# A transpose through TensorE: sixteen ranges with gathered stores in place of eight ranges with direct ones

## The chip, the cores and the metric

The kernel runs on one core of one Trainium2 chip. The metric is the time of one execution on the device, in microseconds; 1264.57 us is the median of 3 runs of the kernel before. Engines are named as in the profile: PE is TensorE (matmuls and transposes, which write PSUM), DVE is VectorE, ACT is ScalarE, POOL is GpSimd, SP is SyncE. DMA engines, 16 of them, move data between main memory (HBM) and the core's own memory (SBUF); SP and ACT issue such transfers, and an engine that issues one does not wait for it.

## The reference

```python
x = np.random.randn(8192, 8192).astype(np.float32)

def reference(x):
    return np.transpose(x)
```

Every float32 of a matrix of 268 MB is read once and written once, and nothing is computed.

## The kernel before

The input is cut into chunks of 128 rows by 4096 columns (2 MiB): `s` is the half of the columns, `c` one of `CH` = 64 groups of rows, and `chunks` lists the `T` = 128 of them, all groups of the first half and then of the second. A load (`load`, L100) brings one chunk to SBUF: 128 partitions, each a 16 KB row of `x`. There are `NIN` = 3 input buffers.

PE turns a chunk into 32 blocks of 128x128 (`transposes`, L111). One transpose takes every fourth column of a range of 512 columns (`B` = 4), so that output partition p holds the output rows 4p to 4p + 3 of that range. A chunk has `NR` = 8 ranges; their results fill PSUM, ranges 0 to 3 in half 0 and 4 to 7 in half 1. PE's program is a loop (L135 to L150) of three chunks a turn, 96 transposes in the code, with semaphores that are counted down.

ACT copies half 0 from PSUM to SBUF, DVE half 1 (L228). They copy straight into the place from which the range will be stored. An output row of 8192 floats is written in pieces, and a piece is longer the more chunks one waits for: each range is collected over `W` = 8 chunks into a region of 16 KB a partition, holding four output rows of 1024 floats, that is 4 KB. The windows of the eight ranges are staggered, so that one range closes in every chunk (`span`, L194) and one store of 2 MiB goes out. Of `NREG` = 9 regions eight are being filled, and one is free or being stored. A window that runs over the end of the first half of the columns is stored in two parts; at the start and the end windows are cut short. These partial stores are of 256 KB to 1792 KB.

`store` (L160) issues on ACT, as `load` does from chunk 3 on (L102): ACT waits until the closing copies are done, issues the store, waits until PE is through with the chunk (L242), and issues the load of three chunks ahead into the buffer that has come free. All DMAs but the first three loads thus stand in ACT's queue, in the order in which ACT reaches them. `wide_dma` (L25) writes the store as an instruction whose source is one contiguous run of 16 KB per partition, while its destination has four rows. PE waits for the load (`s_ld`) and for each PSUM half (`s_bank`); a copy waits for PE (`s_pe`) and, where it opens a window, for the store that last used its region (`s_st`).

Of the kernel before, what the change touches and what calls it, by code (L numbers as in the profile page):

```python
# [24 lines left out]
def wide_dma(nc, eng, queue, out, in_):  # L25


    return eng.add_instruction(
        mybir.InstDMACopy(
            mode="Copy",  # L30
            name=nc.get_next_instruction_name(),
            engine=eng.engine,
            ins=[physical(in_)],
            outs=[physical(out)],
            queue=queue,
        )
    )
# [3 lines left out]
def kernel(  # L41
# [10 lines left out]

    nc = tc.nc
    P = 128
    N, M = x.shape
    assert x.shape == out.shape[::-1]
    dt = x.dtype

    S = 32
    B = 4
    W = 8
    NR = S // B
    NIN = 3
    NREG = 9
    CH = N // P
    J = S * P

    with tc.tile_critical():  # L70
        nc.alloc_sbuf_tensor("pad", [P, 32], dt)
        ident = nc.alloc_sbuf_tensor("ident", [P, P], dt).ap()
        ins = [nc.alloc_sbuf_tensor(f"in{k}", [P, J], dt).ap() for k in range(NIN)]
        SIZE = B * W * P
        regs = nc.alloc_sbuf_tensor("regs", [P, NREG * SIZE], dt).ap()
        NH = NR // 2
        pss = [nc.alloc_psum_tensor(f"ps{k}", [P, NH * B * P], dt).ap() for k in range(2)]

        s_id = nc.alloc_semaphore("s_id")
        s_ld = [nc.alloc_semaphore(f"s_ld{k}") for k in range(NIN)]  # L80
        s_st = [nc.alloc_semaphore(f"s_st{k}") for k in range(NREG)]
        s_bank = [nc.alloc_semaphore("s_banka"), nc.alloc_semaphore("s_bankv")]
        s_pe = nc.alloc_semaphore("s_pe")
        s_cp = [nc.alloc_semaphore("s_cpa"), nc.alloc_semaphore("s_cpv")]

        nc.gpsimd.memset(ident, 0.0).then_inc(s_id, 1)  # L86
        nc.gpsimd.wait_ge(s_id, 1)
# [1 line left out]
            out=ident,  # L89
# [5 lines left out]
            channel_multiplier=1,  # L95
        ).then_inc(s_id, 1)

        chunks = [(s, c) for s in range(M // J) for c in range(CH)]

        def load(t):  # L100
            s, c = chunks[t]
            (nc.sync if t < NIN else nc.scalar).dma_start(  # L102
                out=ins[t % NIN], in_=x[c * P:(c + 1) * P, s * J:(s + 1) * J]
            ).then_inc(s_ld[t % NIN], 16)

        def transposes(k):  # L111
            nc.tensor.sem_inc(s_ld[k], -16).wait_op(s_ld[k], 16, "sem-ge")
            for q in range(NR):
                e, g = divmod(q, NH)
                if g == 0:
                    nc.tensor.sem_inc(s_bank[e], -1).wait_op(s_bank[e], 1, "sem-ge")  # L116
                for b in range(B):
                    tr = nc.tensor.transpose(  # L118
                        pss[e][:, (g * B + b) * P:(g * B + b + 1) * P],
                        ins[k][:, q * B * P + b:(q + 1) * B * P - B + b + 1:B],  # L120
                        ident,
                    )
                if q % 2:
                    tr.then_inc(s_pe, 1)

        T = len(chunks)
        assert T % NIN == NIN - 1
        pe = [nc.tensor.engine]  # L130
        for e in range(2):
            nc.tensor.sem_inc(s_bank[e], 1)
        nc.tensor.wait_ge(s_id, 2)

        turn = nc.alloc_registers("turn", engines=pe)  # L135
        nc.regs_mov(turn, 0)
        nc.br("turns", engines=pe)
        with nc.body("turns", valid_engines=pe):
            now = nc.snap(turn, min_val=0, max_val=T // NIN)
            with nc.tensor.If(now < 3):  # L140
                hint = nc.tensor.mark_branch_hint_location()
            with nc.tensor.If(now > 0):
                transposes(NIN - 1)
            for k in range(NIN - 1):
                transposes(k)
            nc.regs_alu(turn, turn, 1, op=mybir.AluOpType.add)
            nc.tensor.br_lt(
                turn, T // NIN + 1, on_true="turns", on_false="done"
            ).branch_hint(hint)
        nc.switch_bb("done")  # L150

        for t in range(NIN):
            load(t)

        copied = [0, 0]
        free = list(range(NREG))
        stored = [0] * NREG
        window = {}

        def store(q, e, count):  # L160
            t0, r, parts = window.pop(q)
            nc.scalar.wait_ge(s_cp[e], count)
            base = 0
            for s, a, z in parts:
                rows = (z - a) * P
                j0 = s * J + q * B * P
                dst = out[j0:j0 + B * P, a * P:a * P + rows]
                dst = dst.rearrange("(q b) i -> q b i", q=P)
                src = regs[:, r * SIZE + base:r * SIZE + base + B * rows]
                base += B * rows  # L170
                if any(stored):
                    st = wide_dma(nc, nc.scalar, "qActDynamicHW", dst, src)
                else:
                    st = nc.scalar.dma_start(
                        out=dst, in_=src.rearrange("q (b i) -> q b i", b=B)
                    )
                st.then_inc(s_st[r], 16)
                stored[r] += 1
            free.append(r)

        def closes(w, t):
            t0, r, parts = w
            return t + 1 == t0 + sum(z - a for _, a, z in parts)

        for t, (s, c) in enumerate(chunks):
            for e in range(2):
                eng = (nc.scalar, nc.vector)[e]

                place = []
                for q in range(e * NH, (e + 1) * NH):  # L190
                    if q not in window:

                        span = (q - c) % W + 1
                        r = free.pop(0)
                        parts = [(s, c, min(c + span, CH))]
                        if c + span > CH and t + span < T:
                            parts.append((s + 1, 0, c + span - CH))
                        window[q] = (t, r, parts)  # L200
                        if stored[r]:
                            eng.wait_ge(s_st[r], 16 * stored[r])
                    t0, r, parts = window[q]
                    k = [p[0] for p in parts].index(s)
                    base = r * SIZE + B * P * sum(z - a for _, a, z in parts[:k])
                    _, a, z = parts[k]
                    place.append((base + (c - a) * P, (z - a) * P))

                runs = []
                for g in range(NH):  # L210
                    if runs:
                        u = runs[-1]
                        gap = place[g][0] - place[g - 1][0]
                        if place[g][1] == place[u[0]][1] and abs(gap) < 2 ** 15 and (
                            len(u) == 1 or gap == place[u[1]][0] - place[u[0]][0]
                        ):
                            u.append(g)
                            continue
                    runs.append([g])
                for u in runs:  # L220
                    off, dist = place[u[0]]
                    gap = place[u[-1]][0] - place[u[-2]][0] if len(u) > 1 else 0
                    dims = [list(regs.ap[0]), [gap, len(u)], [dist, B], [1, P]]
                    o = bass.AP(regs.tensor, regs.offset + off, dims)
                    i = pss[e][:, u[0] * B * P:(u[-1] + 1) * B * P]
                    i = i.rearrange("p (l b i) -> p l b i", b=B, i=P)
                    eng.wait_ge(s_pe, t * NH + (e * NH + u[-1]) // 2 + 1)  # L227
                    cp = nc.scalar.copy(out=o, in_=i) if e == 0 else nc.vector.tensor_copy(out=o, in_=i)  # L228
                    ends = [e * NH + g for g in u if closes(window[e * NH + g], t)]
                    if ends:  # L230
                        cp.then_inc(s_cp[e], 1)
                        copied[e] += 1
                    if u is runs[-1]:
                        if ends:
                            eng.wait_ge(s_cp[e], copied[e])
                            eng.sem_inc(s_bank[e], 1)
                        else:
                            cp.then_inc(s_bank[e], 1)
                    for q in ends:
                        store(q, e, copied[e])  # L240
            if t + NIN < T:
                nc.scalar.wait_ge(s_pe, (t + 1) * NR // 2)  # L242
                load(t + NIN)
        for r in range(NREG):
            nc.sync.wait_ge(s_st[r], 16 * stored[r])


# [28 lines left out]
```

## Time and profile before

| what | value |
|---|---|
| runs | 1263.68 to 1264.68 us, median 1264.57 |
| the profiled execution's span | 1261.2 us |
| HBM read, written | 268.44 MB each |
| loads: 3 issued by SP, 125 by ACT | 2048 KB each |
| stores | 114 of 2048 KB, and 4 each of 1792, 1536, 1280, 1024, 768, 512 and 256 KB |
| PE transposes | 4096, mean granted clock 0.751 of full speed |
| copies PSUM to SBUF | 256 on ACT, 250 on DVE, of 512 to 2048 columns |

The span runs from the first to the last instruction of one execution that was profiled; the runs time the whole execution. In a row of a group of instructions stand the busy time, the mean duration of one in ns, the idle time of the engine before them, and what ended it. Engine rows of a timeline give the start, the length, and how many were merged.

### The profile page before, as it was taken

What the parts mean: (1) busy time and instruction counts of PE and PEld (TensorE: products, weight loads), DVE (VectorE), ACT (ScalarE), POOL (GpSimd) and SP (SyncE); (2) the same over time, 40 slices, a digit from 0 to 9 for tenths busy, and PEclk for the clock granted to TensorE, in tenths of its full rate; (3) what the DMA queues carried; (4) which work ended last, traced back from release to release, by engine and by line L of the source; (5) the groups of instructions that cost most, each with busy time, mean ns of one, the idle gap of its engine ahead of it and who ended that gap; (6) DMA issues with size and microseconds to landing.
All of it is one profiled execution on the core that took longest, in us unless ns stands there. A gap on an engine that the chain in (4) does not pass through costs nothing. (4 is left out here: it accounts for less than half of the span.)

```text
span 1261.2 us, 9840 instructions
## 1 busy us (share of the span) xinstructions
PE 740.3 (59%) x4096; PEld 719.8 (57%) x4096; DVE 302.7 (24%) x250; ACT 252.6 (20%) x257; POOL 0.7 (0%) x6
## 2 busy tenths in 40 slices
PE   6555655665556565665555655656566655656561
PEld 6555555665556555655555655656566655656561
DVE  3322222222222222222222222222222222222220
ACT  3212121121111211122211121121111211122120
POOL 0000000000000000000000000000000000000000
PEclk9987867777776868687776777676867677777866
DMA  9999999999999999999999999999999999999998
GB/s 386 429 427 426 430 427 429 431 428 430 431 428 431 429 429 430 430 429 430 425 423 419 431 430 429 430 430 429 431 430 429 431 429 430 430 430 429 429 429 351
DMA packets 39273, 536.97 MB, mean 426 GB/s; under 512 B 4320, under 2 KB 4832, under 8 KB 6240
## 3 DMA queue, kind: packets, MB, share of 16 engines
q10 hardware_dynamic: 38832, 530.60, 98.9%
q1 hardware_dynamic: 432, 6.29, 1.2%
q14 instruction: 8, 0.07, 0.0%
q8 instruction: 1, 0.02, 0.0%
HBM read 268.44 MB, written 268.44 MB: 426 GB/s over the span
## 5 line engine op out<-in xcount | busy, mean ns | idle before, releaser
L118 PE MATMUL ps<-ident,in 128*128 128x128 f32 x4096 | 740.3, 363 | 492.9 <-PEq L116 492.9
L118 PEld LDWEIGHTS ps<-ident,in 128*128 128x128 f32 x4096 | 719.8, 220 | 513.2 <-issue 513.2
L228 DVE COPY regs<-ps 128x512 f32<-128x512 f32 (+3 forms) x250 | 302.7, 1246 | 932.4 <-PE ps L118 780.2
L228 ACT COPY regs<-ps 128x512 f32<-128x512 f32 (+3 forms) x256 | 251.3, 1015 | 980.9 <-PE ps L118 495.5
L228 ACT ACT_TABLE_LOAD x1 | 1.3, 1283 | 0.9 <-SPq L70 0.9
L88 POOL TENSOR_SCALAR_AFFINE_SELECT ident<-ident 128x128 f32<-128x128 f32 x1 | 0.3, 292 | 0.2 <-POOL ident L86 0.2
L86 POOL MEMSET ident<- 128x128 f32 x1 | 0.2, 204 | 0.5 <-SPq L70 0.5
L260 POOL MEMSET const-bfloat16-1.0<- 128x1 bf16 x1 | 0.1, 101 | 0.0
L260 POOL MEMSET const-uint8-127<- 128x1 uint8 x1 | 0.1, 101 | 0.0
L260 POOL MEMSET const-float32-0.0<- 128x1 f32 x1 | 0.1, 98 | 0.2 <-issue 0.2
L260 POOL MEMSET const-float32-1.0<- 128x1 f32 x1 | 0.1, 98 | 0.0
## 6 DMA issues: line engine op xcount, KB each, us to landing
in<-in_x_dram ACTq DMA_DIRECT2D x125, 2048.0 KB, 21.7
out_dram<-regs ACTq DMA_DIRECT2D x114, 2048.0 KB, 17.5
out_dram<-regs ACTq DMA_DIRECT2D x4, 1792.0 KB, 17.1
in<-in_x_dram SPq DMA_DIRECT2D x3, 2048.0 KB, 11.6
out_dram<-regs ACTq DMA_DIRECT2D x4, 1536.0 KB, 15.2
out_dram<-regs ACTq DMA_DIRECT2D x4, 1280.0 KB, 15.5
out_dram<-regs ACTq DMA_DIRECT2D x4, 1024.0 KB, 15.6
out_dram<-regs ACTq DMA_DIRECT2D x4, 768.0 KB, 16.5
```

What stands on the lines that cost most here:

```text
L86: nc.gpsimd.memset(ident, 0.0).then_inc(s_id, 1)
L88: nc.gpsimd.affine_select(out=ident, in_=ident, compare_op=mybir.AluOpType.not_equal, fill=1.0, base=0, pattern=[[-1, P]], channel_multipl ...
L118: tr = nc.tensor.transpose(pss[e][:, (g * B + b) * P:(g * B + b + 1) * P], ins[k][:, q * B * P + b:(q + 1) * B * P - B + b + 1:B], ident,)
L228: cp = nc.scalar.copy(out=o, in_=i) if e == 0 else nc.vector.tensor_copy(out=o, in_=i)
L260: nc = _bacc.Bacc("TRN2", target_bir_lowering=False, num_devices=1)
```

## The change

There are now 16 ranges of 256 columns (`B` = 2, `W` = 16): output partition p holds output rows 2p and 2p + 1 of a range, and a store's rows are of 8 KB. Each range is collected over 16 chunks.

- SBUF holds five units of 16 KB a partition (`units`): two input buffers (`NIN` = 2) and three from which ranges are stored (`NF` = 3). The third of these takes the load of chunk 2 and joins the others for window 4.
- Pieces that wait for their range are kept in 120 `slots` of 1 KB a partition. The slots form a triangle: where piece (chunk t, range q) lay, the piece (q, t) is put once the first has been gathered.
- PE takes the ranges of chunk t in the order t, t + 1, ... modulo 16. So the first piece belongs to the range that closes now, the second to the one that closes with the next chunk.
- ACT copies the first piece into the unit that is about to be stored, the second into the next unit, and the other six of half 0 into slots. DVE first gathers the next range, up to 14 pieces, from the slots into its unit (SBUF to SBUF), and then copies half 1 into slots.
- SP issues all DMAs: the store once the last piece and the gather are there, then the load that goes into the input buffer which PE has just finished with.
- After the last chunk, 15 partial ranges are gathered by ACT and DVE in turn and stored, with the input buffers as units too. Partial stores are of 128 KB to 1920 KB.
- PE's loop is written out in line, with 28 transposes of the identity matrix ahead of it.

```diff
-    S = 32
-    B = 4
-    W = 8
-    NIN = 3
-    NREG = 9
+    S, B, W = 32, 2, 16
+    PIECE = B * P
+    SLOTS = W * (W - 1) // 2
+    UNIT = W * PIECE
+    NF = 3
+    NIN = 2
+    WARM = 28
...
-            (nc.sync if t < NIN else nc.scalar).dma_start(
-                out=ins[t % NIN], in_=x[c * P:(c + 1) * P, s * J:(s + 1) * J]
+            nc.sync.dma_start(
+                out=dst, in_=x[c * P:(c + 1) * P, s * J:(s + 1) * J]
...
+        def slot(t, q):
+            t, q = t % W, q % W
+            d = (q - t) % W
+            if d > W // 2 or (d == W // 2 and q < t):
+                t, d = q, W - d
+            return ((d - 1) * W + t) * PIECE
...
+        def gather(e, w, members):
+            eng = (nc.scalar, nc.vector)[e]
+            q, r, _, place, before = w
+            groups = {}
+            for t in members:
+                groups.setdefault(place[t][1], []).append((slot(t, q), place[t][0]))
+            for n, pairs in groups.items():
+                for a, b, da, db, k in runs(pairs):
+                    mv = move(e, view(units, b, db, k, n), view(slots, a, da, k, P))
+            mv.then_inc(s_ga[e], 1)
...
+        for k in range(WARM):
+            nc.tensor.transpose(pss[1][:, :P], ident, ident)
+        now = closing(0)
+        marks = (2, W // 2, W)
+        for t in range(T):
+            src, sem, count = where[t]
+            nc.tensor.wait_ge(sem, count)
+            for i in range(W):
+                if t and i % (W // 2) == 0:
+                    nc.tensor.wait_ge(s_cp[2 * i // W], t)
+                for b in range(B):
+                    o = (i % (W // 2) * B + b) * P
+                    j = (t + i) % W * PIECE + b
+                    tr = nc.tensor.transpose(
+                        pss[2 * i // W][:, o:o + P], src[:, j:j + B * (P - 1) + 1:B], ident
+                    )
+                if i + 1 in marks:
+                    tr.then_inc(s_pe, 1)
...
+            move(0, view(units, off, 0, 1, dist), view(pss[0], 0, 0, 1, P)).then_inc(s_last, 1)
...
+                if nxt[4]:
+                    nc.scalar.wait_ge(s_st[nxt[1]], nxt[4])
+                off, dist = nxt[3][t]
+                move(0, view(units, off, 0, 1, dist), view(pss[0], PIECE, 0, 1, P))
...
+                    if nxt[4]:
+                        nc.vector.wait_ge(s_st[nxt[1]], nxt[4])
+                    for k in range(2):
+                        nc.vector.wait_ge(s_cp[k], t)
+                    gather(1, nxt, members)
...
+            for e in range(2):
+                eng = (nc.scalar, nc.vector)[e]
+                if need:
+                    eng.wait_ge(s_ga[1], need)
+                lo, hi = ((1 if nxt is None else 2), W // 2) if e == 0 else (W // 2, W)
+                eng.wait_ge(s_pe, len(marks) * t + 2 + e)
+                pairs = [(slot(t, t + i), (i - e * (W // 2)) * PIECE) for i in range(lo, hi)]
+                for a, b, da, db, k in runs(pairs):
+                    mv = move(e, view(slots, a, da, k, P), view(pss[e], b, db, k, P))
+                mv.then_inc(s_cp[e], 1)
+            nc.sync.wait_ge(s_last, t + 1)
+            if need:
+                nc.sync.wait_ge(s_ga[1], need)
+            store(now)
+            for u in range(t + 1, T):
+                if after[u] == t:
+                    nc.sync.wait_ge(s_pe, len(marks) * (t + 1))
+                    load(u)
+            now = nxt
+        free += [NF + k for k in range(NIN)]
+        for q in range(W - 1):
+            w = window(q, T - W + 1 + q, T - 1)
+            e = q % 2
+            eng = (nc.scalar, nc.vector)[e]
+            if w[4]:
+                eng.wait_ge(s_st[w[1]], w[4])
+            for k in range(2):
+                eng.wait_ge(s_cp[k], T)
+            gather(e, w, list(w[3]))
+            nc.sync.wait_ge(s_ga[e], gathered[e])
+            store(w)
```

More of the change, by code (lines that the diff above doesn't have):

```diff
@@ L59 @@
     dt = x.dtype
-    S = 32
-    B = 4
-    W = 8
+    S, B, W = 32, 2, 16
     NR = S // B
-    NIN = 3
-    NREG = 9
+    assert NR == W
     CH = N // P
     J = S * P
+    PIECE = B * P
[4 more added lines that the diff above has]
+    WARM = 28
     with tc.tile_critical():
@@ L72 @@
         ident = nc.alloc_sbuf_tensor("ident", [P, P], dt).ap()
[L73 to L77, printed above, removed]
+        units = nc.alloc_sbuf_tensor("units", [P, (NF + NIN) * UNIT], dt).ap()
+        slots = nc.alloc_sbuf_tensor("slots", [P, SLOTS * PIECE], dt).ap()
+        pss = [nc.alloc_psum_tensor(f"ps{k}", [P, UNIT // 2], dt).ap() for k in range(2)]
         s_id = nc.alloc_semaphore("s_id")
-        s_ld = [nc.alloc_semaphore(f"s_ld{k}") for k in range(NIN)]
-        s_st = [nc.alloc_semaphore(f"s_st{k}") for k in range(NREG)]
-        s_bank = [nc.alloc_semaphore("s_banka"), nc.alloc_semaphore("s_bankv")]
+        s_ld = [nc.alloc_semaphore(f"s_ld{k}") for k in range(NIN + 1)]
+        s_st = [nc.alloc_semaphore(f"s_st{k}") for k in range(NF + NIN)]
         s_pe = nc.alloc_semaphore("s_pe")
+        s_last = nc.alloc_semaphore("s_last")
         s_cp = [nc.alloc_semaphore("s_cpa"), nc.alloc_semaphore("s_cpv")]
+        s_ga = [nc.alloc_semaphore("s_gaa"), nc.alloc_semaphore("s_gav")]
+        chunks = [(s, c) for s in range(M // J) for c in range(CH)]
+        T = len(chunks)
         nc.gpsimd.memset(ident, 0.0).then_inc(s_id, 1)
@@ L96, with unit @@
         ).then_inc(s_id, 1)
-        chunks = [(s, c) for s in range(M // J) for c in range(CH)]
+        def unit(k):
+            return units[:, k * UNIT:(k + 1) * UNIT]
+        where = []
+        for t in range(T):
+            if t == NIN:
+                where.append((unit(NF - 1), s_ld[NIN], 16))
+            else:
+                k = (t if t < NIN else t + 1) % NIN
+                n = sum(w[1] is s_ld[k] for w in where)
+                where.append((unit(NF + k), s_ld[k], 16 * (n + 1)))
@@ L100, in load @@
+        after = [None] * T
+        for t in range(NIN + 1, T):
+            after[t] = max(u for u in range(t) if where[u][1] is where[t][1])
         def load(t):
             s, c = chunks[t]
-            (nc.sync if t < NIN else nc.scalar).dma_start(
-                out=ins[t % NIN], in_=x[c * P:(c + 1) * P, s * J:(s + 1) * J]
[L104 to L124, printed above, removed]
@@ L128 @@
[L128 to L149, printed above, removed]
@@ L150 @@
[L150 to L164, printed above, removed]
+            dst, sem, _ = where[t]
+            nc.sync.dma_start(
+                out=dst, in_=x[c * P:(c + 1) * P, s * J:(s + 1) * J]
+            ).then_inc(sem, 16)
@@ new lines, in slot, with runs @@
+        def slot(t, q):
[4 more added lines that the diff above has]
+            return ((d - 1) * W + t) * PIECE
+        def runs(pairs):
+            out = []
+            for a, b in pairs:
+                if out:
+                    g = out[-1]
+                    da, db = a - g[0] - (g[4] - 1) * g[2], b - g[1] - (g[4] - 1) * g[3]
+                    if g[4] == 1 or (da, db) == (g[2], g[3]):
+                        g[2], g[3], g[4] = da, db, g[4] + 1
+                        continue
+                out.append([a, b, 0, 0, 1])
+            return out
@@ new lines, in view, with move, window @@
+        def view(base, offset, step, n, dist):
+            dims = [list(base.ap[0]), [step, n], [dist, B], [1, P]]
+            return bass.AP(base.tensor, base.offset + offset, dims)
+        def move(e, o, i):
+            return nc.scalar.copy(out=o, in_=i) if e == 0 else nc.vector.tensor_copy(out=o, in_=i)
+        free = list(range(NF - 1))
+        stored = [0] * (NF + NIN)
+        def window(q, t0, t1):
+            r = free.pop(0)
+            parts, place, base = [], {}, r * UNIT
+            for s in sorted({chunks[t][0] for t in range(t0, t1 + 1)}):
+                mine = [t for t in range(t0, t1 + 1) if chunks[t][0] == s]
+                n = len(mine) * P
+                for k, t in enumerate(mine):
+                    place[t] = (base + k * P, n)
+                parts.append((s, chunks[mine[0]][1], chunks[mine[-1]][1] + 1, base))
+                base += B * n
+            return q, r, parts, place, 16 * stored[r]
@@ L165, in store @@
+        def store(w):
+            q, r, parts, _, _ = w
+            for s, a, z, base in parts:
                 rows = (z - a) * P
                 j0 = s * J + q * B * P
[L167 to L170, printed above, removed]
+                dst = out[j0:j0 + B * P, a * P:z * P].rearrange("(p b) i -> p b i", p=P)
+                src = units[:, base:base + B * rows]
@@ L171, in store @@
                 if any(stored):
-                    st = wide_dma(nc, nc.scalar, "qActDynamicHW", dst, src)
+                    st = wide_dma(nc, nc.sync, "qSPDynamicHW", dst, src)
                 else:
-                    st = nc.scalar.dma_start(
-                        out=dst, in_=src.rearrange("q (b i) -> q b i", b=B)
+                    st = nc.sync.dma_start(
+                        out=dst, in_=src.rearrange("p (b i) -> p b i", b=B)
                     )
@@ L179, in store @@
             free.append(r)
[L181 to L185, printed above, removed]
+        gathered = [0, 0]
+        def gather(e, w, members):
[8 more added lines that the diff above has]
+            mv.then_inc(s_ga[e], 1)
+            gathered[e] += 1
@@ new lines, in closing @@
+        def closing(t):
+            return window(t % W, max(0, t - W + 1), t) if t < T else None
+        for t in range(NIN + 1):
+            load(t)
+        nc.tensor.wait_ge(s_id, 2)
+        for k in range(WARM):
+            nc.tensor.transpose(pss[1][:, :P], ident, ident)
+        now = closing(0)
+        marks = (2, W // 2, W)
+        for t in range(T):
+            src, sem, count = where[t]
[11 more added lines that the diff above has]
+                    tr.then_inc(s_pe, 1)
+            q, r, parts, place, before = now
+            if before:
+                nc.scalar.wait_ge(s_st[r], before)
+            nc.scalar.wait_ge(s_pe, len(marks) * t + 1)
+            off, dist = place[t]
+            move(0, view(units, off, 0, 1, dist), view(pss[0], 0, 0, 1, P)).then_inc(s_last, 1)
+            need = gathered[1]
+            nxt = None
+            if t + 1 < T:
+                if t + 1 == NIN + 2:
+                    free.append(NF - 1)
+                while not free:
+                    raise RuntimeError
+                nxt = closing(t + 1)
+            if nxt:
+                if nxt[4]:
+                    nc.scalar.wait_ge(s_st[nxt[1]], nxt[4])
+                off, dist = nxt[3][t]
+                move(0, view(units, off, 0, 1, dist), view(pss[0], PIECE, 0, 1, P))
+            if nxt:
+                members = [u for u in nxt[3] if u < t]
+                if members:
+                    if nxt[4]:
[3 more added lines that the diff above has]
+                    gather(1, nxt, members)
@@ L186 @@
             for e in range(2):
                 eng = (nc.scalar, nc.vector)[e]
[L189 to L244, printed above, removed]
+                if need:
[5 more added lines that the diff above has]
+                    mv = move(e, view(slots, a, da, k, P), view(pss[e], b, db, k, P))
@@ L245 @@
+        for r in range(NF + NIN):
             nc.sync.wait_ge(s_st[r], 16 * stored[r])
```

## The prediction

> **What bounds the kernel now.** I read the page of the profile first, then the waits, then the stages, then the end of the timeline.
>
> ```profile
> span 1261.2 us, 9840 instructions
> PE 740.3 (59%) x4096; PEld 719.8 (57%) x4096; DVE 302.7 (24%) x250; ACT 252.6 (20%) x257; POOL 0.7 (0%) x6
> DMA  9999999999999999999999999999999999999998
> DMA packets 39273, 536.97 MB, mean 426 GB/s; under 512 B 4320, under 2 KB 4832, under 8 KB 6240
> q10 hardware_dynamic: 38832, 530.60, 98.9%
> q14 instruction: 8, 0.07, 0.0%
> q8 instruction: 1, 0.02, 0.0%
> ```
>
> The 16 DMA engines are busy in every slice, while PE is at 59% and the copying engines at 24% and 20%. So the time is the sum of the packets, and a change is worth what it does to packets or to DMA idleness. The two instruction rows say that code loading takes DMA time too, and that there is little of it now.
>
> ```profile
> ACT regs L228 <- PE ps L118: 495.5, 100, 9.2
> ACT regs L228 <- DMA out_dram<-regs: 473.9, 60, 10.4
> DVE regs L228 <- DMA out_dram<-regs: 152.1, 23, 7.8
> ```
>
> These waits are those of engines that wait for the DMA, and cost nothing. The stages confirm it (columns: stretch, its length, busy time of PE, weight load, DVE, ACT and POOL, granted clock, DMA share, GB/s):
>
> ```profile
> 20.00:30.00 10.00, 8.07 (x53) 7.73 (x52) 3.68 (x6) 3.93 (x7) 0.00 (x0) 0.83 0.98 397
> 740.00:1200.00 460.00, 278.36 (x1511) 270.77 (x1512) 110.20 (x76) 91.41 (x84) 0.00 (x0) 0.74 1.01 430
> 1250.00:1262.00 12.00, 0.00 (x0) 0.00 (x0) 0.00 (x0) 0.00 (x0) 0.00 (x0) 0.50 0.52 218
> ```
>
> At 430 GB/s one chunk (2 MiB in, 2 MiB out) takes 9.75 us, and 128 of them 1248 us. In the trace's DMA records all gaps together are 4.9 us per engine, of which 2.9 lie in the last stretch, where some engines end up to 4.5 us before the slowest. The profiled span is 1261.2, the median of the runs 1264.57: 3.4 us lie around the span, and I carry them over unchanged.
>
> ```profile
> 1227.95 5.26 PE L118 MATMUL ps<-ident,in 128*128 128x128 f32 x32 [3.19 <-PEq L116]
> 1232.63 2.48 DVE L228 COPY regs<-ps 128x512 f32<-128x512 f32 x4 [6.51 <-DMA out_dram<-regs]
> 1232.97 0.79 ACTq L28 DMA_DIRECT2D out_dram<-regs  x1
> 1234.50 14.89 ACTq L28 DMA_DIRECT2D out_dram<-regs  x5
> ```
>
> The last chunk is transposed by 1233.2, and the last stores are issued while the queue is still full: the DMA never waits for compute at the end.
>
> **The change part by part.**
>
> *Longer store rows.* The number of 16 KB packets does not change: a store's packet is one partition's 16 KB, cut into four rows of 4 KB now and two of 8 KB then. In the DMA records a load packet takes 611 ns; of a store's eight packets per engine two take 611 and six 616. Packets overlap by 4 and 3 ns, so 607 against 613. Partial stores also have four rows per packet: 315 ns for 8 KB, 541 for 14 KB, so 75.3 per 2 KB and 13.6 fixed at 616; a load has 8.6 fixed, and the 512 B packets of the first store, one row each, 27 ns, so 8.2 fixed. It is the number of rows that costs, not the direction: three extra rows 5 ns by the records, 6 with the overlap. Two fewer rows save 3.3 to 4.0 ns on six packets, 20 to 24 ns per store, 128 times: **-2.6** us (bounds 0, if the first store's row misleads, and -3.1).
>
> *More partial stores.* Ranges filled over 16 chunks instead of 8 make 15 partial sizes, four of each, instead of 7: 158 stores instead of 142. The bytes are the same. Each extra store has 8 packets per engine at 13.6 ns fixed less 3.5 of overlap, and a 9 ns semaphore packet: 0.09 us, times 16: +1.4; the first store has 256 packets of 512 B fewer, -0.1. **+1.3** (1.2 to 1.4).
>
> *PE's loop is unrolled.* Before, PE runs 96 transposes in a loop; after, 4124 stand in line, each a weight load and a matmul, with 127 more waits: 8,400 instructions. ACT, DVE and SP go from 1012 instructions in the trace (633, 357, 22) to about 2010, counted in the built program. The price is in the records: the one 16 KB instruction packet took 1005 ns, and the data packet behind it 1106 instead of 611, so 1.5 us of one DMA engine; the eight 8 KB packets took 309 each, and the packet behind them 185 to 430 too much. From ACT's and DVE's 990 instructions in eight 8 KB packets, an instruction is about 64 bytes; PE then needs 33 packets of 16 KB, 50 us of DMA engine time, 3.1 us for each of 16 if they are spread; the others' 8 more packets at 0.65 add 0.3. **+3.4.** Lower bound: their bytes alone at 430 GB/s, 1.3. Upper: the DMA records show that after a fetch has shifted an engine more packets come late (after the one at 97 us a packet of 1412 ns and two of 667 and 728), doubling it: 7. Nothing hides this, since every DMA engine is busy; PE itself should not wait, as 256 instructions last it four chunks. [...] The trace has only nine such packets, but each delayed a data packet, so I go by the row.
>
> *The start.* Only two store units exist until chunk 3, and ACT's second piece copy (line 245) waits for the store two windows back, which SP's one queue carries behind the loads. Going through it with rows (first packet 1.0 us after issue, a landing seen 0.6 us later, 4.87 us per 2 MiB, PE 4.11 per chunk at full clock, ACT 1.44 for 1536 columns, DVE about 2.4 per half chunk): store 0 lands at 18.6; ACT frees PSUM half 0 at 20.4, so chunk 2 starts 2.2 us after its load; store 1 lands at 24.1, and chunk 3 ends at 30.05 instead of 27.6. Its end releases load 5, whose first packet comes at 31.1, when the queue ran dry at 30.45: 0.65 idle; with chunk 3 at 5.57 us (clock 0.83, as one chunk had there) 2.1. From chunk 5 on there are three units and the queue keeps ahead. **+1.0** (0 to 2.1). The 28 warming transposes run before the first load has landed at 8.43, and cost nothing.
>
> *The middle.* Per chunk, VectorE gains a gather of 14 pieces, 3584 columns. From its PSUM copies (684 ns for 512, 2291 for 2048: 1.05 ns a column and 0.15 per instruction) that is 4.1 us, and with the half chunk of 2.3 it is 6.4 of 9.75. Behind the gather stands the copy that frees PSUM half 1; before it, the wait for the store of three windows ago. The gather may start when the last chunk is copied, about when the next load lands, and its store is not needed until 9.75 us later: 5 us to spare. ACT has 0.4 + 0.4 + 1.4. With two input buffers a load is issued once PE is done with the chunk, 0.6 + 5.8 + 1.0 = 7.4 us after the landing's packets, when the queue still holds store, load, store: 14.6 us. SP issues (0.56 and 0.4 us) carry all DMAs in one order, with ACT freed of them. **0**; were the gather to take over 7.4 us, VectorE would be the bound. [...]
>
> *The end.* After load 127 there remain two full stores, 9.76 us of queue, and then 15 partial stores that need a gather first. From the end of that load: 0.6 to PE, 5.8 for its chunk (740.3 / 128), 2.3 + 0.1 for VectorE's half, then ACT's gather of 15 pieces in two copies (1865 for 2048, about 1650 for 1792: 3.5 us), 1.1 to the first packet: 13.5. The queue is empty for **+3.8** us (2.0 with PE at 4.1 us, 5.0 with PE at 6.5 and slower copies). Later gathers take at most 4.1 us each on two engines in turn, and their stores 4.6 down to 0.3 us each, with five units for them, so the gathers keep ahead.
>
> Sum: -2.6 + 1.3 + 3.4 + 1.0 + 0 + 3.8 = +6.9: span 1268.1, median **1271.5**. Low ends: -3.1 + 1.2 + 1.3 + 0 + 2.0 = +1.4 (1266.0). High ends: 0 + 1.4 + 7 + 2.1 + 5.0 = +15.5 (1280.1).
>
> **Rivals.**
> 1. Code loading costs nothing: its packets only take what the faster DMA engines have over, since those end up to 4.5 us ahead of the slowest. Then +3.5: 1268.1; with the end's low bound of 2.0 too, +1.7: 1266.3. A change within 0.2% (2.5 us) is what a measurement of this kernel can't tell from none. [...]
> 2. Faster. In phase, the engines' packets slow each other: 30 packets of 760 to 1020 ns at 21.7 to 23 us, clusters at 87, 117 and 685 us, in all about 3 us per engine. If half as many rows of double length end these clusters, this gains 3 and the rows 3.1; if code loading is hidden, the start loses nothing and the end's gap is 2.0, the balance is -3.1 - 3 + 1.3 + 2.0 = -2.8: 1261.8. It decides from a store packet at 611 with no clusters. Against it: steady packets already run at 607 and 613, so there is little left to win.
> 3. VectorE becomes the bound: a gather above 7.4 us. At 8.2 (twice the row) a chunk takes 10.5, +0.75 x 112 = +84: about 1349.
> 4. All of PE's code comes through one DMA engine: +50, about 1315. Against it: the nine packets seen held up packets of several engines.
>
> **How the numbers follow.** The forecast with its own range 1266 to 1280 gets 0.50, rival 1 0.28 (0.20 of it within 0.2%), rival 2 0.12, rivals 3 and 4 0.05 each. Faster 0.12, same 0.20, slower 0.68. The range 1263 to 1281 takes in half of rival 2 and leaves out 3 and 4 and little more.
>
> **What would show it.** Right: DMA at 9 in all middle slices; instruction rows of some 0.6 MB; store packets at 611 to 613; one hole of about 4 us after the last chunk, ended by ACT's gather; loads waiting for PE only in the first 40 us. Wrong: holes in the middle, gathers far from 4.1 us, no growth of the instruction rows, or a rate in the middle above 432 GB/s.

## The result and the profile after

The changed kernel takes 1275.48 us (median of 4 runs, 1274.58 to 1278.37) against 1264.55: a ratio of 1.0092, 95% interval 1.0078 to 1.0106. It is slower by 10.9 us where 6.9 were forecast, inside the stated range. The same kernel, run again on another occasion beside the later experiments, had a ratio of 1.0118 (1.0095 to 1.0141).

The page of the profile after: the span, the engines, the DMA share in 40 slices, and the queues (packets, MB, share of 16 engines).

```profile
span 1272.8 us, 10293 instructions
PE 741.8 (58%) x4124; PEld 717.1 (56%) x4124; DVE 581.1 (46%) x528; ACT 283.5 (22%) x396; POOL 0.7 (0%) x6
DMA  9999999999999999999999999999999999999979
GB/s 375 359 427 430 428 428 431 430 428 428 427 429 429 431 433 427 432 431 429 429 428 426 422 413 427 428 429 430 428 432 429 428 433 429 429 430 430 430 331 396
q1 hardware_dynamic: 41312, 536.89, 99.4%
q8 instruction: 32, 0.52, 0.1%
q14 instruction: 14, 0.11, 0.0%
```

The DMA is still the bound: nines everywhere but one slice. Two places are new: the second slice (359 GB/s) and the last but one (331). The instruction rows have grown from 9 packets to 46, 0.63 MB. The 32 packets of 16 KB among them are called code packets below.

The same by stretches (length, busy time of PE, weight load, DVE, ACT, POOL, granted clock, DMA share, GB/s):

```profile
30.00:40.00 10.00, 6.44 (x42) 6.28 (x41) 3.89 (x6) 3.80 (x5) 0.00 (x0) 0.83 0.77 304
40.00:50.00 10.00, 5.51 (x38) 5.13 (x38) 6.58 (x8) 2.56 (x5) 0.00 (x0) 0.92 0.93 312
740.00:1200.00 460.00, 275.80 (x1504) 266.87 (x1504) 216.01 (x195) 98.01 (x141) 0.00 (x0) 0.74 1.01 429
1220.00:1230.00 10.00, 6.63 (x32) 6.45 (x32) 3.06 (x2) 2.81 (x3) 0.00 (x0) 0.67 0.66 280
1230.00:1240.00 10.00, 0.00 (x0) 0.00 (x0) 3.94 (x5) 8.19 (x6) 0.00 (x0) 0.50 0.63 265
```

There are holes at the start and at the end, and the long middle runs at 429 instead of 430. The DMA records give the difference per engine:

- Idle time is 11.1 us against 3.7 before: 3.3 of it at 30 to 41 us and 7.2 at 1219 to 1234. The kernel before has 3.2 at its end, where the faster engines are done ahead of the slowest. Idle time is counted here between any two packets of an engine, whatever they carry, and behind its last one until the slowest engine is done. (The prediction has 4.9 for the kernel before.)
- Instruction packets take 2.2 us against 0.2.
- What packets of 16 KB took beyond 616 ns, called late time below, is 8.2 us against 3.0. Of this growth 2.1 us lie at 20 to 50 us.
- Rows and partial stores together come to -3.1 us: 10,121 packets of 616 ns are now 611, which is 3.2, and the additional partial stores, less what packets overlap, take back 0.1.

These terms add up to +11.5 us, and the span grew by 11.6.

The waits (us in total, times, longest) show that no engine on the compute side became the bound, and how much is waited for stores:

```profile
DVE slots L151 <- PE ps L220: 629.7, 126, 12.5
PE ps L220 <- DMA units<-in_x_dram: 475.5, 124, 5.7
DVE units L151 <- DMA out_dram<-units: 37.8, 8, 6.7
ACT units L151 <- DMA out_dram<-units: 34.5, 8, 5.4
```

PE waits for loads, as it should where the DMA binds; VectorE, although it gathers, waits 630 us for PE. The waits of ACT and VectorE for stores fell from 474 and 152 us to 35 and 38; all of them lie in the first 33 us or behind the last chunk. The timeline at the start:

```profile
26.67 0.37 ACT L151 COPY units<-ps 128x256 f32<-128x256 f32 x1 [0.95 <-PE ps L220]
30.64 0.33 SPq L122 DMA_DIRECT2D units<-in_x_dram  x1
32.31 0.37 ACT L151 COPY units<-ps 128x256 f32<-128x256 f32 x1 [5.26 <-DMA out_dram<-units]
34.16 7.47 PE L220 MATMUL ps<-ident,units 128*128 128x128 f32 x48 [3.56 <-ACT slots L151]
39.74 0.33 SPq L122 DMA_DIRECT2D units<-in_x_dram  x1
```

Load 5 goes out at 30.64, when the queue has run dry at 30.45 on the first engines. ACT then stands until 32.31 for store 2, so PE starts chunk 4 only at 34.16 and load 6 goes out at 39.74, when the first engines have been dry since 38.6. Store 2 was that late because of one DMA engine. The first code packet of PE came at 24.0 us (931 ns); of the next packets of that engine, the one right behind it took 1115 ns and two later ones 1122 and 1379, and it finished load 4 at 30.97 where the other fifteen had at 28.3 to 28.7. The code packet and the one behind it account for 1.4 us of this; what made the two later packets long is not shown.

The timeline at the end:

```profile
1220.07 6.63 PE L220 MATMUL ps<-ident,units 128*128 128x128 f32 x32 [3.37 <-DMA units<-in_x_dram]
1226.81 2.29 DVE L151 COPY slots<-ps 128x2048 f32<-128x2048 f32 x1 [7.71 <-PE ps L220]
1229.21 8.98 ACT L151 COPY units<-slots 128x2048 f32<-128x2048 f32 x6 [3.71 <-DVE slots L151]
1239.12 1.56 DVE L151 COPY units<-slots 128x2048 f32<-128x2048 f32 x2 [6.06 <-DMA out_dram<-units]
```

The chunk, the copy, then ACT's gather from 1229.21: the queue starts again at 1233.9. The slowest DMA engine had been done at 1229.5, a hole of 4.5 us for it; the faster ones had already idled between the last two full stores, the first of them from 1219.8 to 1223. From 1239 on the gathers wait for free units, so they keep ahead.

### The profile page after: what moved, and what is told of

Same layout as the page of the kernel before. It is cut to its first block, busy times and chain, and to the rows that moved or that the text cites. A ratio compares the mean times of both kernels' runs of the same rounds, so it can differ in the third digit from the quotient of the medians.

```text
span 1272.8 us, 10293 instructions
## 1 busy us (share of the span) xinstructions
PE 741.8 (58%) x4124; PEld 717.1 (56%) x4124; DVE 581.1 (46%) x528; ACT 283.5 (22%) x396; POOL 0.7 (0%) x6
## 4 chain that ended last, share of the span: by engine, by line
DMA 69%; PE 28%; ACT 1%; issue 1%; DVE 0%; ACTq 0%; SPq 0%; DVEq 0%
DMA units<-in_x_dram 65%; PE ps L220 28%; DMA out_dram<-units 4%; ACT units L151 1%; DVE slots L151 0%; ACT slots L151 0%; DVE units L151 0%; ACTq L287 0%; DVEq L263 0%; SPq L318 0%; SPq L74 0%; ACTq L230 0%
## 5 line engine op out<-in xcount | busy, mean ns | idle before, releaser
L220 PE MATMUL ps<-ident,units 128*128 128x128 f32 x4096 | 735.7, 361 | 483.2 <-DMA units<-in_x_dram 475.5
L220 PEld LDWEIGHTS ps<-ident,units 128*128 128x128 f32 x4096 | 711.3, 219 | 507.6 <-DMA units<-in_x_dram 499.1
L151 DVE COPY slots<-ps 128x512 f32<-128x512 f32 (+6 forms) x232 | 300.0, 1331 | 629.7 <-PE ps L220 629.7
L151 DVE COPY units<-slots 128x1792 f32<-128x1792 f32 (+7 forms) x296 | 281.3, 997 | 54.5 <-DMA out_dram<-units 37.8
L151 ACT COPY units<-ps 128x256 f32<-128x256 f32 x255 | 82.8, 375 | 734.5 <-PE ps L220 722.6
L151 ACT COPY slots<-ps 128x1536 f32<-128x1536 f32 x128 | 184.4, 1441 | 221.9 <-PE ps L220 221.9
L151 ACT COPY units<-slots 128x2048 f32<-128x2048 f32 (+4 forms) x12 | 15.4, 1326 | 26.3 <-DMA out_dram<-units 22.6
L207 PE MATMUL ps<-ident 128*128 128x128 f32 x28 | 6.1, 415 | 1.7 <-POOL ident L94 1.7
L207 PEld LDWEIGHTS ps<-ident 128*128 128x128 f32 x28 | 5.8, 227 | 1.7 <-POOL ident L94 1.7
## 6 DMA issues: line engine op xcount, KB each, us to landing
units<-in_x_dram SPq DMA_DIRECT2D x128, 2048.0 KB, 13.8
out_dram<-units SPq DMA_DIRECT2D x4, 1280.0 KB, 11.5
```

The lines of the kernel that those rows point to most:

```text
L151: return nc.scalar.copy(out=o, in_=i) if e == 0 else nc.vector.tensor_copy(out=o, in_=i)
L207: nc.tensor.transpose(pss[1][:, :P], ident, ident)
L220: tr = nc.tensor.transpose(pss[2 * i // W][:, o:o + P], src[:, j:j + B * (P - 1) + 1:B], ident)
```

## The experiments

Each ratio is to the kernel before, run beside it. Late time and idle time are per DMA engine, from the DMA records of one profile.

### PE's code in line, in the kernel before

```diff
-        with nc.body("turns", valid_engines=pe):
...
-            for k in range(NIN - 1):
-                transposes(k)
...
+        for t in range(T):
+            transposes(t % NIN)
```

> The kernel before, with PE's loop written out in line and nothing else changed. Theory A (code loading takes DMA engine time, and each packet of it makes data packets behind it late): the 16 KB instruction packets go from 1 to about 32, 2 us per DMA engine by themselves and 1 to 2 in late packets, so +3 to +4 us against the kernel before, no hole in the DMA. Theory B (code loading is hidden, and the late packets of the changed kernel come from its store addresses): within 1 us of the kernel before, late packets as in it, about 3 us per engine.

1267.14 us, ratio 1.0028 (1.0018 to 1.0038): +3.7 us. Its queues, and the middle:

```profile
q10 hardware_dynamic: 38832, 530.60, 98.6%
q8 instruction: 33, 0.54, 0.2%
740.00:1200.00 460.00, 275.89 (x1504) 268.31 (x1504) 110.38 (x76) 91.46 (x84) 0.00 (x0) 0.74 1.01 429
```

There are 33 code packets in place of one (2.0 us per engine), late time is 3.8 instead of 3.0, and idle time 4.8 instead of 3.7, with nearly all of the growth at 1227 to 1230 us and no hole at the start. Code loading by itself cost here what theory A gave it, though late packets are the smallest part of it.

### The end's first gather done ahead

```diff
-                nxt = closing(t + 1)
+            nxt = closing(t + 1) if t + 1 < T else window(0, T - W + 1, T - 1)
...
-        for q in range(W - 1):
+        nc.sync.wait_ge(s_cp[0], T)
+        nc.sync.wait_ge(s_ga[1], gathered[1])
+        store(now)
+        for q in range(1, W - 1):
```

> The changed kernel; the first of the 15 ranges left at the end is gathered and stored as in the chunks before, so that its store stands in the queue right behind that of the last chunk. Theory A (the 4.5 us hole at the end is the wait for the last chunk's copies and one gather): the hole closes, -4.5 us against the changed kernel, 1271. Theory B (gathers on two engines can't keep the queue full): the hole moves behind the first of these stores, 0 to -1 us.

1275.65 us, ratio 1.0090 (1.0073 to 1.0107). The stretches around the last chunk's end:

```profile
1220.00:1230.00 10.00, 6.71 (x35) 6.52 (x34) 4.39 (x3) 2.08 (x3) 0.00 (x0) 0.67 0.78 334
1230.00:1240.00 10.00, 3.35 (x18) 3.16 (x16) 6.12 (x5) 4.90 (x4) 0.00 (x0) 0.67 1.00 425
```

The hole behind the last chunk is closed (265 GB/s became 425), and its cause was the one named. The time shows little of it: idle time fell from 11.1 to 7.9, but late time was 13.1 in this profile against 8.2. Against the changed kernel as run again (1.0118, late time 12.6, idle time 11.1) the gain is 3.5 us, with intervals that overlap; between these two profiles idle time is 3.2 us less and the span 3.1 us shorter (1274.7 against 1277.8). So the cause of the hole is shown; a price of some 3 us is what two profiles say, and the runs alone don't establish it.

### Three store units from the start

```diff
-            if t == NIN:
-                where.append((unit(NF - 1), s_ld[NIN], 16))
-            else:
-                k = (t if t < NIN else t + 1) % NIN
...
-        free = list(range(NF - 1))
+        free = list(range(NF))
...
-        for t in range(NIN + 1):
+        for t in range(NIN):
             load(t)
```

> The changed kernel; all three store units are free from the start, and only two loads go out ahead of chunk 0 instead of three. Theory A (the two holes at 30 to 41 us come from waits on the store two windows back): both go, 3.7 us, and 0.4 to 1 us of new dryness comes at 13 us, where load 2 now waits for PE: -3 us against the changed kernel, 1272.5. Theory B (the holes come from one late DMA engine behind a code packet): at least the second hole stays, 0 to -1 us, or the loss moves to the first 20 us.

1282.35 us, ratio 1.0141 (1.0118 to 1.0163): worse. Its start:

```profile
28.29 5.58 PE L217 MATMUL ps<-ident,units 128*128 128x128 f32 x32 [4.35 <-DMA units<-in_x_dram]
33.90 0.33 SPq L119 DMA_DIRECT2D units<-in_x_dram  x1
30.00:40.00 10.00, 8.25 (x56) 7.67 (x55) 4.37 (x7) 3.53 (x4) 0.00 (x0) 0.89 0.80 279
```

No engine waits for a store any more in that stretch, and a hole is still there, as theory B had it: after a code packet at 20.0 us one engine is some 2.8 us behind, PE waited 4.35 us for load 3, and load 5 went out at 33.90 into a queue that most engines had found dry since 32. The waits for stores are thus not needed for the hole. That the code packet alone is enough is not shown: it took 0.9 us, long data packets make up part of the 2.8, and a second engine without a code packet was 1.4 us behind. That the code packet is needed was not tried either: no version has a start without one.

### PE in a loop, in the changed kernel

```diff
+        for t in range(W):
+            transposes(t)
...
+        with nc.body("turns", valid_engines=pe):
...
+            for t in range(W, 2 * W):
+                transposes(t)
```

> The changed kernel with PE in a loop of 16 chunks (1090 instructions, 70 KB) behind 16 chunks in line; ACT and VectorE wait for their own last copy and count PE's semaphore up by an instruction of its own, some 0.1 us per chunk beside the path. Theory A (code loading and what it delays): if the loop stays loaded, 16 KB instruction packets fall from 32 to 8 to 10, and the time by 2 to 3.5 us against the changed kernel, 1272 to 1273.5; the late packets per engine fall from 8.2 us towards 4. Theory B (late packets come from the store addresses): only the code's own 1.3 us go, late packets stay near 8. If the loop is too long to stay loaded, the instruction packets stay at 32 and the time at 1275.5 by both.

1278.23 us, ratio 1.0114 (1.0097 to 1.0131). The code packets went:

```profile
q8 instruction: 8, 0.13, 0.0%
q14 instruction: 16, 0.13, 0.0%
```

The long loop stayed loaded: no code packet of PE between 217 and 1199 us. Yet late time was 13.8, and 6.1 of it fell between 740 and 1200 us. So theory A is wrong for the late packets: they do not come from loading PE's code. Both theories had the time fall below 1275.5 us; it was 1278.23, inside what the changed kernel shows by itself. The holes at the start stayed, since the first turn is still in line (a code packet at 24.0).

### The changed kernel once more, without most of the gather, and other copies in the kernel before

> The changed kernel unaltered, beside the other runs of this group on the same chip, as their yardstick: about 1.009 of the kernel before. Its late packets (over 616 ns, summed per DMA engine) were 8.2 us in its first profile; if they vary from run to run by several us, single profiles of the variants so far can't be ranked by them.

1278.46 us (1276.33 to 1282.06). Late time 12.6 where the first profile had 8.2, the difference between 740 and 1200 us (5.2 against 1.8): the same kernel varies by 4 us in this.

```diff
             for n, pairs in groups.items():
+                if 24 <= gathered[1] < 126:
+                    pairs = pairs[:1]
                 for a, b, da, db, k in runs(pairs):
```

> The changed kernel; from the 25th gather to the last one before the tail, each gather copies only the first piece of each of its parts, so most of what is stored there is left over from before, while every DMA and every wait stays. VectorE's work from SBUF to SBUF falls from 2.4 to about 0.3 us per chunk. Theory C (the copies from SBUF to SBUF make DMA packets late): late packets between 200 and 1200 us fall to the level of the kernel before, 1 us per engine, and the time by 3 to 6 us against the changed kernel. Theory D (the late packets come from where the DMAs read and write in HBM, and from code loading): late packets and time as in the changed kernel, within 1.5 us.

1277.68 us, ratio 1.0110 (1.0087 to 1.0133), late time 13.1. VectorE's gathers in it, and ahead of them those of the changed kernel as run again (busy, mean ns, idle before):

```profile
L151 DVE COPY units<-slots 128x1792 f32<-128x1792 f32 (+7 forms) x296 | 281.2, 996 | 54.6 <-DMA out_dram<-units 38.0 <-DVE slots L151 0.5
```

```profile
L151 DVE COPY units<-slots 128x256 f32<-128x256 f32 (+7 forms) x170 | 81.5, 498 | 55.5 <-DMA out_dram<-units 39.2
```

200 us less work for VectorE, and neither the time nor the late packets changed. And the counterpart:

```diff
+            for k in range(4):
+                nc.vector.wait_ge(s_more, 4 * t + k + 1)
+                a, b = (0, 1024) if k % 2 else (1024, 0)
+                nc.vector.tensor_copy(
+                    out=more[:, a:a + 1024], in_=more[:, b:b + 1024]
+                ).then_inc(s_more, 1)
```

> The kernel before; VectorE copies 1024 columns from SBUF to SBUF four times per chunk behind its own copies, about 2.8 us of its idle time, the same kind and amount as the gather. Theory C: late packets rise from 3 to 6 us or more per engine and the time by 3 us or more. Theory D: no change, within 1 us of the kernel before.

1267.93 us, ratio 1.0053 (1.0025 to 1.0082): the time moved as theory C had it (3 us or more), not as theory D did (within 1 us). With 354 us of such copies, late time is 3.2, as without them. Five of the ten times lie at 1265.8 to 1266.4, some 2.4 us over the kernel before; the other five lie at 1269.4 to 1281.1. The one profile (span 1264.2) is of the first five; of its 3.0 us over the kernel before 2.7 are idle time (6.4 against 3.7), nearly all of it from 1227 us on. Nothing on record explains the other five, and whether they had more late packets is not known. So it is the run without most of the gather that rules theory C out for the late packets of the changed kernel; this one profile agrees.

### Store rows of 2 KB

```diff
+                if rows == W * P:
+                    dst = out[j0:j0 + B * P, a * P:z * P].rearrange("r (c i) -> r c i", i=512)
```

> The changed kernel with the full stores described in rows of 2 KB instead of 8 KB, at the same addresses and in the same order: eight rows per 16 KB packet instead of two. Theory A (each extra row costs a packet 1.7 to 2.0 ns): six more rows, store packets near 622 ns on six of eight, +6 us against the changed kernel. Theory B (only the number of packets counts, rows cost nothing): store packets stay at 611, no change.

1287.68 us, ratio 1.0191 (1.0174 to 1.0208), 9.2 us over the changed kernel beside it. In the DMA records 10,615 packets took 626 ns instead of 611, 10 us per engine. With the two kernels' 611 (two rows) and 616 (four), a row beyond the second costs a packet 2.5 ns, and the second nothing, if a load's packet of one row (611) may stand for a store's. Theory A's kind is right, its size was 1.7 to 2.0.

### Another place in HBM, and a shallower queue

```diff
-                    j = (t + i) % W * PIECE + b
+                    j = (t + i) % W * PIECE + b * P
...
-                        pss[2 * i // W][:, o:o + P], src[:, j:j + B * (P - 1) + 1:B], ident
+                        pss[2 * i // W][:, o:o + P], src[:, j:j + P], ident
...
-                dst = out[j0:j0 + B * P, a * P:z * P].rearrange("(p b) i -> p b i", p=P)
+                dst = out[j0:j0 + B * P, a * P:z * P].rearrange("(b p) i -> p b i", p=P)
```

> The changed kernel with output partition p holding rows p and p + 128 of a range instead of 2p and 2p + 1: the same packets of two 8 KB rows, but the two rows lie 4 MiB apart in HBM instead of 32 KiB, and partitions 32 KiB apart instead of 64. Theory D1 (the late packets of the second half come from where stores fall in HBM): the late packets between 740 and 1200 us change clearly from the 5.2 us of the changed kernel beside which this one runs, to under 2 or over 8, and the time with them by 3 us or more. Theory D2 (they come from the order and depth of the queue, two loads ahead instead of three): they stay at 2 to 6 us, the time at 1.009 to 1.012 of the kernel before.

1276.69 us, ratio 1.0108 (1.0080 to 1.0136); late time 12.2, of it 3.0 between 740 and 1200 us. That is inside what the changed kernel shows by itself (1.8 and 5.2), so this change of addresses does nothing that can be told.

```diff
-    NIN = 3
+    NIN = 2
```

on top of the first experiment's kernel.

> The kernel before with PE's loop in line, as in the first experiment, and two input buffers in place of three, so that a load is issued one chunk later; store rows of 4 KB as before. Theory D2: late packets between 740 and 1200 us rise from 0.5 towards 2 to 6 us and the time to 1270 or more. Theory D1: they stay under 1 us, and the time within 2 us of 1267, plus up to 2 us at the start.

1386.42 us, ratio 1.0950 (1.0919 to 1.0982). Its page:

```profile
span 1385.6 us, 9621 instructions
GB/s 340 394 381 373 373 418 377 399 367 367 417 348 396 412 377 418 394 377 406 392 421 375 403 365 397 408 364 402 363 390 419 366 391 361 375 420 378 410 412 374
PE ps L118 <- PEq L116: 605.8, 127, 8.5
```

Against the first experiment, late time rose from 3.8 to 76 us and idle time from 4.8 to 51: the queue that ran dry here cost more in late packets than in idleness. This went far beyond what D2 expected, since here the queue was dry in the middle (20 us of idle time from 740 to 1200 us), which it is not in the changed kernel (0.1 us). So it shows that late packets came with the short queue of this kernel, and not that the changed kernel's few have this cause.

### End and loop together

Both diffs above in one kernel.

> The changed kernel with both the end's first gather done ahead and PE in a loop of 16 chunks. If holes and code packets add up in the time, -4.5 and -1.4: about 1.006 of the kernel before. If late packets take back what is won (each of the two changes alone ended near 1.009 to 1.011), 1.009 again, with late packets of 12 us per engine or more.

1277.32 us, ratio 1.0103 (1.0084 to 1.0123): code packets 8, idle time 9.9, late time 14.2. That is the second of the two outcomes expected: what is won in idleness and code does not show in the time. The best ratio of any version of the changed kernel is the 1.0090 above.

## Why the prediction was right, and where its sizes were wrong

The direction, the bound and the places were right: every middle slice at 9, 0.63 MB of code, a hole behind the last chunk ended by ACT's gather. Two of the signs that the prediction names came out otherwise: the gather took 2.4 us, not 4.1, and SP waited for PE ahead of 125 loads throughout the run (454.5 us in all), not only in the first 40 us, though the queue did not run dry by it in the middle. That the time lies inside the range owes something to luck: the late packets, 5.2 us in one profile and 9.6 in the other, stand in the sum almost only as an upper bound of the code term, for a cause that the loop experiment rules out.

- Longer store rows: -2.6 forecast (0 to -3.1), 3.2 us by the packets, since all full ones are at 611. The model (5 ns for three extra rows, evenly) was off: a packet of two rows took 611 ns, as a load's of one row did.
- More partial stores: +1.3 forecast. Together with the rows they come to -3.1, so they cost about 0.1: all partial packets have two rows instead of four as well (most of 2 KB took 89 ns before and 84 after), which the term left out.
- PE's loop unrolled: +3.4 forecast, +3.7 measured in the kernel before. PE indeed waits hardly longer than in its loop (495 us against 493 in all), but with 33 code packets the kernel took 0.28% longer, where the DMA share is 1.01 from 740 to 1200 us.
- The start: +1.0 forecast (0 to 2.1), 3.3 us of idle time in two holes, and 2.1 us of late time beside it. The first hole is there as worked out (queue dry at 30.45 forecast and measured; first packet of load 5 at 31.1 forecast, 31.6 measured). The second hole was not foreseen, because I had priced the code packets as an even 1/16 for each engine: one of 16 engines was 2.3 us late, in part by a code packet, and of the 16 landing updates of load 4 the last came at 31.32 us, the others by 28.95; of those of store 2, for which ACT waited until 32.31, the last at 32.28 and the others by 29.98.
- The middle: 0 forecast. The gather was faster than its term had it: from SBUF, VectorE's 2048 columns took 1227 ns, against 2292 from PSUM, 1.87 times as fast.

```profile
L151 DVE COPY slots<-ps 128x2048 f32<-128x2048 f32 x64 | 146.7, 2292 | 319.3 <-PE ps L220 319.3
L151 DVE COPY units<-slots 128x2048 f32<-128x2048 f32 x60 | 73.6, 1227 | 20.6 <-DMA out_dram<-units 12.8 <-DVE slots L151 0.5
```

- What the step for the middle left out is the late packets, and this is the largest miss: over the whole run 5.2 us more than before in the first profile and 9.6 in the second, of it 3.3 and 6.6 between 200 and 1200 us. Their cause is open: not PE's code loading, not VectorE's copies, not, as far as tried, the addresses of the stores. Depth of the queue remains, argued from one much coarser run. That all transfers now stand in SP's queue instead of ACT's was not tried by itself.
- The end: +3.8 forecast (its addends make 13.4 rather than 13.5, and so 3.6). It was 4.5 for the slowest DMA engine, and 4.0 more idle time than before on the average of the 16. PE's chunk took 6.6 us at a clock of 0.67 instead of the mean of 5.8.

Of the rivals, code loading for nothing is ruled out, VectorE as the bound and code through one engine as well. The faster case needed clusters of late packets to go; late time grew from 3.0 to 8.2 us. That engines in phase slow each other, as it has it, is inferred from such clusters.

## What to carry to other kernels

Where the DMA engines are busy all the time, count what a change adds to them that is no data: here the written-out code was loaded by the same engines (33 packets, 2.0 us per engine and 3.7 us of time in the kernel before), and in the changed kernel store 2 landed at 32.28 us with the one engine of 16 that was 2.3 us late, in part by such a packet. A deeper queue may hide that: with three input buffers, the kernel before with its code in line met a code packet at 28.0 us and idled 0.2 us in its first 60; the changed kernel, with two, idled 3.6, and the kernel before with two 2.9. How much of this is the code packet's is not shown. Buffers given up for longer rows are taken from just this depth. And a transfer's rows were worth 0.25% here (3.2 us), from 4 KB to 8 KB: less than the hole of 4.5 us that the longer drain at the end left.

## What was not expected of the hardware

- Packets with which the DMA engines started together after a hole were slow: in the changed kernel, of the 29 packets of 16 KB that started in the 0.8 us from 31.5 and from 40.6 us on, after the two holes, 25 took 1058 to 1531 ns instead of 611. That the engines hinder each other there is inferred.
- The engines drifted apart, in the changed kernel by 4.8 us between the fastest and the slowest at the last full store but one, though few packets are long: between 740 and 1200 us, of some 12,000 packets of 16 KB, 14 took over 625 ns in the kernel before, and 190 and 484 in two profiles of the changed one.
- Two input buffers instead of three made the kernel before 9.5% slower, with PE busy for 55% of the time.
